# Weight-block sums in a seven-product stage: adding transfers that read DRAM, and another order of the products

## The chip, the core and the metric

The kernel runs on one core of a Trainium2 chip. The core has a matrix engine (TensorE, PE in the profile, with PEld for its weight loads), a vector engine (VectorE, DVE), a scalar engine (ScalarE, ACT), GpSimd (POOL), SyncE (SP), and 16 DMA engines that they all share. Each engine works through its own instructions in order and waits on semaphores for the others. The metric is the device time of one execution in microseconds.

## The reference, cut to what matters

With `DEPTH = 1` the model has one layer: a short gated convolution as token mixer, then a routed mixture of experts. The change lies in the mixer's first product, `h @ w_in`, of 2048 tokens by 1024 channels with a matrix of 1024 by 3072.

```python
def short_conv_mixer(h, w_in, conv_w, w_out):
    gate_b, gate_c, v = jnp.split(h @ w_in, 3, axis=-1)
    return (gate_b * dwconv_centred(gate_c * v, conv_w)) @ w_out

hl = modulate(rms_norm(lat, norm_g[i, 0]), sh1, sc1)
yl = short_conv_mixer(hl, sc_w_in[j], sc_conv[j], sc_w_out[j])
lat = lat + g1 * yl
hl2 = modulate(rms_norm(lat, norm_g[i, 1]), sh2, sc2)
lat = lat + g2 * expert_choice_ffn(hl2, moe_router[i], moe_w_gate[i], moe_w_up[i], moe_w_down[i])
```

## The kernel before

Every float32 factor of a product is split into a high part, rounded to the type `F32R`, and a low part, the rest. A product of two such factors is three matmuls: high by high, low by high, high by low. Tokens go in four quarters of 512 (`QT`).

The first two quarters are multiplied plainly (`in_mm`). The last two are multiplied in a **seven-product stage**, which is the place of the change. It runs over 12 units. A unit takes two column tiles of 128 columns, that is two pieces of `w_in`: piece a and piece b, of 1024 rows by 128 columns each. Their two row halves are (a, 0), (a, 1), (b, 0) and (b, 1), blocks of 512 rows by 128 columns. These four blocks and the four blocks of activations (two quarters by two halves of the channels) form a product of 2 by 2 blocks, which is done with seven block products of sums and differences in place of eight. The seven activation blocks have the names `B11, T1, T2, B21, T3, B22, T4`; they were summed earlier, written to the DRAM scratch `fscr`, and are loaded (tile `fu`) and split (tile `tg`) once for all units, in `refill`, by 14 half groups whose order is `halves`.

One block product is 12 matmuls (`product`): four row tiles, three matmuls each, into one bank of PSUM (`pm`, 128 by 512). In step n of the stage (n = 7 u + i, for product i of unit u) the code writes, in this order: `make_block(n + 4)`, which makes the weight block that is needed four products later (`AHEAD = 4`); whatever `later` holds for step n, mostly parts of the convolution of the unit before (`conv_start`, `conv_rest`, `conv_gate`); in each fourth step an `ada_step`, a slice of another matrix-vector sum (load of `aw` by POOL, addition into `acc` by DVE); and `unit_step`, the product itself and what moves its bank. No scheduler changes this order: each engine takes its instructions as they are written.

`make_block` writes the tile `sb`, whose part 0 is the high part and part 1 the low part. It works on the loaded pieces (`raw`, three buffers, `n_raw`), in place: DVE forms a sum or difference in one half of a piece (L780 to L785), ACT rounds it into part 0 (L786), and the low part is done in one of two ways. For the blocks that need no sum (the unit's products 0, 1 and 4) ACT writes the negated high part into part 1 (L788) and POOL issues a DMA that adds the float32 block from `raw` to it (L789). For the other four DVE subtracts (L791). When the last block of a piece is made, `piece_done` gives its buffer back, and SP issues the load of the piece three further on (L200). The load waits until everything that reads or writes the buffer is through.

The products of a unit share banks: `st[(0, 1, 2, 1, 4, 1, 2)[i]]`. Product 0 keeps a bank for itself until the unit's end, products 1, 3 and 5 add up in a second, 2 and 6 in a third, 4 has a fourth. After products 1, 2, 3 and 5 ACT copies the bank's running sum into one of four quarters of the results x and y (tiles `cx`, `cy`, L847), and a product that goes on in the same bank waits for that copy. DVE adds the rest: one sum after product 4 (L849), three after product 6 (L851 to L853).

Of the kernel before, what the change touches and what calls it, by code (L numbers as in the profile page):

```python
# [13 lines left out]
ALU = mybir.AluOpType  # L14
# [8 lines left out]
KD = D // P  # L23
# [13 lines left out]
N_GROUP = 7  # L37
# [3 lines left out]
def dram(src, offset, ap):  # L41
    return bass.AP(tensor=src.tensor, offset=src.offset + offset, ap=ap)
# [3 lines left out]
def block_kernel(ctx: ExitStack, tc, x, c, ada_w, ada_b, norm_g, w_in, conv, w_out, router, wg, wu, wd, out):  # L46
    nc = tc.nc
# [130 lines left out]
    pieces, n_load, n_high, n_done = [], 6, 6, 6  # L178
# [179 lines left out]
    with tc.tile_pool(name="mix", bufs=1) as mix, ExitStack() as ctx_mixd:  # L358
# [13 lines left out]
        def wide(name, shape=[P, 2 * QT + 4], dt=F32):  # L372
            return cvp.tile(shape, dt, name=name, tag="wide", bufs=6)
# [252 lines left out]
        for g in range(4):  # L626
# [3 lines left out]
            full = scale_x(0, k)  # L630
# [9 lines left out]
            full = scale_x(0, k + 1)  # L640
# [43 lines left out]
            if t + 1 < KD:  # L684
                ada_load(g, t + 1, eng)

        T4, B11, T1, T2, B21, T3, B22 = range(N_GROUP)
        group_of_k = {(2, 0): B11, (2, 1): B21, (3, 1): B22}
        rows_F = {}

# [18 lines left out]
        def save_sums(j):  # L709
# [3 lines left out]
            for h in range(2):  # L713
# [12 lines left out]

        grp, full_of = {}, {}

        halves = [(T4, 0), (T4, 1), (B11, 0), (B11, 1), (T1, 0), (T1, 1), (B21, 0), (B21, 1), (T3, 0), (T3, 1),
                  (T2, 0), (T2, 1), (B22, 0), (B22, 1)]  # L730
        in_big = [(T4, 0), (T4, 1), (B11, 0), (B11, 1), (T1, 0), (T2, 0), (T2, 1), (B22, 0)]

        def load_full(s):
            if s >= len(halves):
# [26 lines left out]
        def raw_half(i, h):  # L761
            return raws[i][:, 4 * h:4 * h + 4]

        def piece_done(i):
            nonlocal n_high, n_done
            raws.pop(i)
            n_high = n_done = i + 1
            load_to(i + depth())
# [3 lines left out]
        def make_block(n):  # L772

            u, i = divmod(n, N_GROUP)
            a, b = first_s + 2 * u, first_s + 2 * u + 1
            t = blk[n] = hl_tile([P, 2, KD // 2, P], name="sb")
            p, h = ((b, 1), (a, 0), (b, 1), (b, 1), (a, 1), (a, 0), (b, 0))[i]
            full = raw_half(p, h)
            if i == 2:
                nc.vector.tensor_add(full, raw_half(b, 0), full)  # L780
            elif i == 3:
                nc.vector.tensor_sub(full, full, raw_half(a, 0))
            elif i == 5:
                nc.vector.tensor_sub(full, full, raw_half(b, 0))
                nc.vector.tensor_sub(raw_half(b, 0), raw_half(a, 1), raw_half(b, 1))  # L785
            nc.scalar.activation(t[:, 0], full, AF.Copy)  # L786
            if i in (0, 1, 4):
                nc.scalar.activation(t[:, 1], t[:, 0].bitcast(F32), AF.Copy, scale=-1.0)  # L788
                nc.gpsimd.dma_start(t[:, 1], full, accum_op=ALU.add)  # L789
            else:  # L790
                nc.vector.tensor_sub(t[:, 1], full, t[:, 0].bitcast(F32))  # L791
            if i > 4:
                piece_done(p)

        def product(o, n, first):
            t, g = blk.pop(n), n % N_GROUP
            for j in range(KD // 2):
                r = grp[g, j]
                last = j == KD // 2 - 1
                nc.tensor.matmul(o, t[:, 0, j], r[:, 0], start=(first and j == 0), stop=False, skip_group_check=True)  # L800
                nc.tensor.matmul(o, t[:, 1, j], r[:, 0], start=False, stop=False, skip_group_check=True)  # L801
                nc.tensor.matmul(o, t[:, 0, j], r[:, 1], start=False, stop=last, skip_group_check=True)  # L802
# [29 lines left out]
        def unit_step(u, i, st):  # L832

            n = N_GROUP * u + i
            if i in (0, 1, 2, 4):
                st[i] = mm.tile([P, QT], F32, name="pm", tag="mm")
            o = st[(0, 1, 2, 1, 4, 1, 2)[i]]
            product(o, n, i in (0, 1, 2, 4))
            if i == 1:
                st["x"] = wide("cx")  # L840
            if i == 2:
                st["y"] = wide("cy")
            x, y = st.get("x"), st.get("y")
            q0, q1 = slice(2, 2 + QT), slice(2 + QT, 2 + 2 * QT)
            if i in (1, 2, 3, 5):
                dst = {1: (x, q0), 2: (y, q1), 3: (x, q1), 5: (y, q0)}[i]
                nc.scalar.activation(dst[0][:, dst[1]], o, AF.Copy)  # L847
            elif i == 4:
                nc.vector.tensor_add(x[:, q0], x[:, q0], o)  # L849
            elif i == 6:  # L850
                nc.vector.tensor_add(y[:, q1], y[:, q1], y[:, q0])  # L851
                nc.vector.tensor_add(y[:, q0], y[:, q0], st[0])
                nc.vector.tensor_add(x[:, q1], x[:, q1], o)  # L853
                (m, ct), (_, ct2) = units[u]
                if m == 0:
                    at(n + 1, lambda: conv_gate(ct, x))
                    at(n + 2, lambda: conv_gate(ct2, y))
                else:
                    convs[ct] = x
                    at(n + 1, lambda: conv_start(ct, x, y))  # L860
                    at(n + 2, lambda: conv_rest(ct, x, y))
# [4 lines left out]
        for i, (ct, q) in enumerate(steps):  # L866
# [10 lines left out]
            for k in range(KD):  # L877
# [14 lines left out]
                if i < 5 and k % 2 == 1:  # L892
                    t = 4 * i + k // 2
# [28 lines left out]
        st = {}  # L922
# [16 lines left out]
        for n in range(n_steps):  # L939
            u, i = divmod(n, N_GROUP)  # L940
# [709 lines left out]
```

## Time and profile before

| | |
|---|---|
| median of 3 runs | 1893.7 us (1890.02 to 1894.17) |
| profiled execution | 1893.85 us, span of its instructions 1892.1 us |
| seven-product stage in it | first matmul at 313.85 us, last at 570.06 us |
| busy over the span | PE 1819.7 us, DVE 1198.5, ACT 893.0, POOL 338.5 |
| mean granted TensorE clock | 0.986 of full |

The profile is of one execution. Times of engines overlap, so busy times don't add up to the span. A matmul's recorded length is longer than its share of the engine, since matmuls are pipelined: what counts is the distance from one start to the next. An idle time in brackets is followed by the instruction that ended it. The stretch of 313.6 to 570.3 us is one seventh of the execution. Of the page's 40 slices TensorE is below 80% busy in the first, the last and the seventeenth (757 to 804 us, where tokens are given to experts); the stage lies in none of them.

### The profile page before, as it was taken

The numbers are of one execution on the slowest core, as the hardware profiler recorded it, in microseconds if no ns is written. First come the engines' busy times: TensorE is split into PE (matmuls) and PEld (weight loads), VectorE is DVE, ScalarE is ACT, GpSimd is POOL, SyncE is SP. The second block draws the span as 40 slices with busy tenths as digits, with TensorE's granted clock in tenths as the row PEclk, the third lists the DMA queues.
The fourth block names the chain that finished last, engine by engine and source line by source line (L and its number), as shares of the span: only waits on it lengthen the run. The fifth ranks groups of instructions, "written<-read, shape, count | busy, mean of one in ns | idle before, by whom it ended". The sixth has DMA issues, their size and how long they took to land.

```text
span 1892.1 us, 29374 instructions
## 1 busy us (share of the span) xinstructions
PE 1819.7 (96%) x11511; PEld 1612.5 (85%) x11511; DVE 1198.5 (63%) x1686; ACT 893.0 (47%) x1190; POOL 338.5 (18%) x514
## 2 busy tenths in 40 slices
PE   7999999998999999499999999999999999999997
PEld 6778887876777888398899999999999999999996
DVE  6554347666667777778656666765666676566653
ACT  4512335433344555566444553544455355445541
POOL 1112232122212222210102102110210221021002
PEclk9999999999999999799999999999999999999999
DMA  9354367656568888386787878788787978877774
GB/s 334 111 190 129 110 226 243 156 139 156 138 170 265 246 261 244 134 258 192 202 251 246 233 223 267 215 244 245 252 228 224 264 221 245 244 250 230 224 229 83
DMA packets 309818, 403.11 MB, mean 213 GB/s; under 512 B 103300, under 2 KB 174256, under 8 KB 309680
## 3 DMA queue, kind: packets, MB, share of 16 engines
q1 hardware_dynamic: 282336, 314.16, 54.4%
q0 software_dynamic: 27344, 87.08, 17.0%
q8 instruction: 90, 1.47, 0.3%
q14 instruction: 48, 0.39, 0.1%
HBM read 311.52 MB, written 57.68 MB: 195 GB/s over the span
## 4 chain that ended last, share of the span: by engine, by line
PE 75%; DMA 7%; DVE 7%; issue 5%; ACT 3%; POOL 1%; SPq 0%; POOLq 0%; DVEq 0%; ACTq 0%
PE pm L1473 11%; PE pm L1475 11%; PE pm L1477 11%; PE pm L1542 6%; PE pm L1540 6%; PE pm L1541 6%; PE pm L488 3%; PE pm L489 3%; PE pm L491 3%; PE pm L1002 3%; PE pm L1003 3%; PE pm L1005 3%; DMA sb<-raw 2%; DMA raw<-in_sc_w_in_dram 1%; DMA tr<-xs 1%
## 5 line engine op out<-in xcount | busy, mean ns | idle before, releaser
L235 DVE TENSOR_TENSOR ws<-raw,ws 128x1024 fp32r<-128x1024 f32 x408 | 485.0, 1221 | 281.5 <-ACT ws L225 281.4
L225 ACT ACTIVATE ws<-raw 128x1024 fp32r<-128x1024 f32 x408 | 412.6, 1051 | 413.4 <-PE pm L1477 323.4
L1473 PE MATMUL pm<-xT,ws 128*128 128x256 f32 x2048 | 568.4, 278 | 0.4 <-ACT xT L1452 0.4
L1475 PE MATMUL pm<-xT,ws 128*128 128x256 f32 x2048 | 567.0, 277 | 1.9 <-DVE xT L1453 1.7
L1477 PE MATMUL pm<-xT,ws 128*128 128x256 f32 x2048 | 566.6, 277 | 0.0
L1475 PEld LDWEIGHTS pm<-xT,ws 128*128 128x128 f32 x2048 | 385.6, 188 | 3.9 <-DVE xT L1453 2.1
L1473 PEld LDWEIGHTS pm<-xT,ws 128*128 128x128 f32 x2048 | 385.2, 188 | 2.0 <-ACT xT L1452 0.8
L1477 PEld LDWEIGHTS pm<-xT,ws 128*128 128x128 f32 x2048 | 385.1, 188 | 0.0
L1570 POOL DMA_INDIRECT out_dram<-ot,idx x30 | 104.7, 3491 | 588.0 <-DVE ot L1559 583.9
L1542 PE MATMUL pm<-ws,hT 128*128 128x512 f32 x504 | 198.4, 394 | 0.0
L1540 PE MATMUL pm<-ws,hT 128*128 128x512 f32 x504 | 198.1, 393 | 0.0
L1541 PE MATMUL pm<-ws,hT 128*128 128x512 f32 x504 | 197.0, 391 | 0.0
L488 PE MATMUL pm<-hl,ws 128*128 128x512 f32 x384 | 154.0, 401 | 0.0
L489 PE MATMUL pm<-hl,ws 128*128 128x512 f32 x384 | 150.7, 392 | 0.0
L800 PE MATMUL pm<-tg,sb 128*128 128x512 f32 x336 | 135.2, 402 | 15.3 <-ACT cx L847 15.2
L801 PE MATMUL pm<-tg,sb 128*128 128x512 f32 x336 | 132.6, 395 | 0.7 <-DMA sb<-raw 0.7
L802 PE MATMUL pm<-tg,sb 128*128 128x512 f32 x336 | 132.3, 394 | 0.0
L1542 PEld LDWEIGHTS pm<-ws,hT 128*128 128x128 f32 x504 | 94.7, 188 | 20.0
L1541 PEld LDWEIGHTS pm<-ws,hT 128*128 128x128 f32 x504 | 94.7, 188 | 19.8
L1540 PEld LDWEIGHTS pm<-ws,hT 128*128 128x128 f32 x504 | 94.7, 188 | 18.7
L491 PE MATMUL pm<-hl,ws 128*128 128x512 f32 x384 | 108.1, 390 | 0.0
L1002 PE MATMUL pm<-ws,hl 128*128 128x512 f32 x256 | 101.8, 398 | 0.8 <-ACT hl L933 0.8
(362 smaller groups left out, 2507.4 us busy)
## 6 DMA issues: line engine op xcount, KB each, us to landing
raw<-in_moe_w_down_dram SPq DMA_DIRECT2D x128, 512.0 KB, 4.6
raw<-in_moe_w_gate_dram SPq DMA_DIRECT2D x126, 512.0 KB, 4.9
raw<-in_moe_w_up_dram SPq DMA_DIRECT2D x126, 512.0 KB, 3.9
raw<-in_sc_w_in_dram SPq DMA_DIRECT2D x42, 512.0 KB, 4.6
xt<-in_x_dram SPq DMA_DIRECT2D x32, 512.0 KB, 6.5
sb<-raw POOLq DMA_DIRECT2D x36, 256.0 KB, 3.9
hl<-in_ada_w_dram SPq DMA_DIRECT2D x32, 256.0 KB, 6.3
aw<-in_ada_w_dram SPq DMA_DIRECT2D x16, 512.0 KB, 5.4
```

Of the source, the lines that this page charges most:

```text
L225: nc.scalar.activation(t[:, 0], raws[n_high], AF.Copy)
L235: (eng or nc.vector).tensor_sub(t[:, 1, ..., s], raw[..., s], t[:, 0, ..., s].bitcast(F32))
L488: nc.tensor.matmul(ps[m], wh, t[:, 0], start=(k == 0), stop=False)
L489: nc.tensor.matmul(ps[m], wl, t[:, 0], start=False, stop=False)
L491: nc.tensor.matmul(ps[m], W(k, m)[0], t[:, 1], start=False, stop=(k == KD - 1))
L1002: nc.tensor.matmul(ps[h], vh[:, k], w[:, 0, half(h)], start=(k == 0), stop=False)
L1473: nc.tensor.matmul(o, w[:, 0, j, c0], xT[:, 0, k], start=(k == 0 and f % 2 == 0), stop=False, skip_group_check=True)
L1475: nc.tensor.matmul(o, w[:, 0, j, c0], xT[:, 1, k], start=False, stop=False, skip_group_check=True)
L1477: nc.tensor.matmul(o, w[:, 1, j, c0], xT[:, 0, k], start=False, stop=(k == KD - 1), skip_group_check=True)
L1540: nc.tensor.matmul(ps[s], h, w[:, 0, j], start=(k == 0), stop=False)
L1541: nc.tensor.matmul(ps[s], h, w[:, 1, j], start=False, stop=False)
L1542: nc.tensor.matmul(ps[s], l, w[:, 0, j], start=False, stop=(k == KD - 1))
```

## The change

`make_block`, `unit_step` and two lists are rewritten; the arithmetic of the stage is the same, in another order.

- The adding DMA of a block without a sum reads the block from `w_in` in DRAM, no longer from the loaded piece. Its source is then four runs of 128 floats for each partition in place of one run of 512 floats.
- The order of the seven products is B11, T1, T2, B21, T3, B22, T4 (it was T4, B11, T1, T2, B21, T3, B22). Their weight blocks are (a, 0); the sum (b, 0) + (b, 1), formed in (b, 0); that minus (a, 0); (a, 1); (b, 1) minus the sum, formed in (a, 0); (a, 1) minus the sum, formed in (b, 0); and (b, 1). Blocks 0, 3 and 6 are those without a sum.
- Three banks in place of four: products 0, 2, 4 and 6 add up in one, 1 and 5 in a second, 3 has a third. ACT copies after products 0, 1, 2, 4 and 6 (five copies, were four), DVE adds after 3, 4 and 5 (three, were four).
- `halves` and `in_big` follow the new order. Loads of pieces are asked for at the same steps as before: after block 5 (piece a) and block 6 (piece b).

```diff
-        T4, B11, T1, T2, B21, T3, B22 = range(N_GROUP)
+        B11, T1, T2, B21, T3, B22, T4 = range(N_GROUP)
...
-        halves = [(T4, 0), (T4, 1), (B11, 0), (B11, 1), (T1, 0), (T1, 1), (B21, 0), (B21, 1), (T3, 0), (T3, 1),
-                  (T2, 0), (T2, 1), (B22, 0), (B22, 1)]
-        in_big = [(T4, 0), (T4, 1), (B11, 0), (B11, 1), (T1, 0), (T2, 0), (T2, 1), (B22, 0)]
+        halves = [(B11, 0), (B11, 1), (T1, 0), (T1, 1), (T2, 0), (T2, 1), (B21, 0), (B21, 1), (T3, 0), (T3, 1),
+                  (B22, 0), (B22, 1), (T4, 0), (T4, 1)]
+        in_big = [(B11, 0), (B11, 1), (T1, 0), (T1, 1), (T2, 0), (B22, 0), (B22, 1), (T4, 0)]
...
-            p, h = ((b, 1), (a, 0), (b, 1), (b, 1), (a, 1), (a, 0), (b, 0))[i]
+            p, h = ((a, 0), (b, 0), (b, 0), (a, 1), (a, 0), (b, 0), (b, 1))[i]
             full = raw_half(p, h)
-            if i == 2:
-                nc.vector.tensor_add(full, raw_half(b, 0), full)
-            elif i == 3:
+            if i == 1:
+                nc.vector.tensor_add(full, full, raw_half(b, 1))
+            elif i == 2:
                 nc.vector.tensor_sub(full, full, raw_half(a, 0))
+            elif i == 4:
+                nc.vector.tensor_sub(full, raw_half(b, 1), raw_half(b, 0))
             elif i == 5:
-                nc.vector.tensor_sub(full, full, raw_half(b, 0))
-                nc.vector.tensor_sub(raw_half(b, 0), raw_half(a, 1), raw_half(b, 1))
+                nc.vector.tensor_sub(full, raw_half(a, 1), full)
+                piece_done(a)
             nc.scalar.activation(t[:, 0], full, AF.Copy)
-            if i in (0, 1, 4):
+            if i in (0, 3, 6):
+                src, offset, ap, _ = pieces[p]
                 nc.scalar.activation(t[:, 1], t[:, 0].bitcast(F32), AF.Copy, scale=-1.0)
-                nc.gpsimd.dma_start(t[:, 1], full, accum_op=ALU.add)
+                nc.gpsimd.dma_start(t[:, 1], dram(src, offset + h * (KD // 2) * ap[1][0], [ap[0], [ap[1][0], KD // 2], ap[2]]),
+                                    accum_op=ALU.add)
             else:
                 nc.vector.tensor_sub(t[:, 1], full, t[:, 0].bitcast(F32))
-            if i > 4:
-                piece_done(p)
+            if i == 6:
+                piece_done(b)
...
-            if i in (0, 1, 2, 4):
+            if i in (0, 1, 3):
                 st[i] = mm.tile([P, QT], F32, name="pm", tag="mm")
-            o = st[(0, 1, 2, 1, 4, 1, 2)[i]]
-            product(o, n, i in (0, 1, 2, 4))
-            if i == 1:
-                st["x"] = wide("cx")
-            if i == 2:
-                st["y"] = wide("cy")
+            o = st[(0, 1, 0, 3, 0, 1, 0)[i]]
+            product(o, n, i in (0, 1, 3))
+            if i < 2:
+                st["xy"[i]] = wide("c" + "xy"[i])
...
-            if i in (1, 2, 3, 5):
-                dst = {1: (x, q0), 2: (y, q1), 3: (x, q1), 5: (y, q0)}[i]
+            if i in (0, 1, 2, 4, 6):
+                dst = {0: (x, q0), 1: (y, q1), 2: (x, q1), 4: (y, q0), 6: (y, q0)}[i]
                 nc.scalar.activation(dst[0][:, dst[1]], o, AF.Copy)
+            if i == 3:
+                nc.vector.tensor_add(x[:, q0], x[:, q0], o)
             elif i == 4:
-                nc.vector.tensor_add(x[:, q0], x[:, q0], o)
+                nc.vector.tensor_add(y[:, q1], y[:, q1], y[:, q0])
+            elif i == 5:
+                nc.vector.tensor_add(x[:, q1], x[:, q1], o)
             elif i == 6:
-                nc.vector.tensor_add(y[:, q1], y[:, q1], y[:, q0])
-                nc.vector.tensor_add(y[:, q0], y[:, q0], st[0])
-                nc.vector.tensor_add(x[:, q1], x[:, q1], o)
```

How the change stands on the engines, at the places that matter. First SP, the loads of four pieces in the middle of the stage, with the semaphores that each waits for (`DMASW` counts DMAs that POOL issued, `DMAHW` those of SP). Before:

```order
L200 DMA raw_2910<-in_sc_w_in_dram 128x8x128 [waits DMAHW0_49,DMAHW4_49,DMASW3_49,DVE_49]
L200 DMA raw_2932<-in_sc_w_in_dram 128x8x128 [waits DMAHW5_49,DMAHW1_49,DVE_49]
L200 DMA raw_3048<-in_sc_w_in_dram 128x8x128 [waits DMAHW6_49,DMASW0_49,DVE_49]
L200 DMA raw_3074<-in_sc_w_in_dram 128x8x128 [waits DMAHW0_49,DVE_49]
```

and the same four loads with the change:

```order
L200 DMA raw_2907<-in_sc_w_in_dram 128x8x128 [waits DMAHW0_49,DMAHW4_49,DVE_49,Activation_49]
L200 DMA raw_2932<-in_sc_w_in_dram 128x8x128 [waits DMAHW1_49,DMAHW5_49,DVE_49,Activation_49]
L200 DMA raw_3044<-in_sc_w_in_dram 128x8x128 [waits DMAHW6_49,DVE_49,Activation_49]
L200 DMA raw_3073<-in_sc_w_in_dram 128x8x128 [waits DMAHW0_49,DVE_49,Activation_49]
```

Before, every second load waits for a DMA of POOL; with the change none does, and each waits for ACT and DVE.

Then ACT, from step 1 of the third unit on. L786 rounds a block and L788 negates it, L847 copies a bank. Before (the first row is block 5, the fourth and fifth are block 0 of the next unit):

```order
L786 ACTIVATE sb<-raw 128x512 [waits DVE_49,PE_49]
L847 ACTIVATE cx<-pm 128x512 [waits PE_49]
L786 ACTIVATE sb<-raw 128x512 [waits DMASW0_49,DVE_49]
L847 ACTIVATE cy<-pm 128x512 [waits DMASW2_49,PE_49]
L786 ACTIVATE sb<-raw 128x512 [waits DMAHW0_49,DMASW2_49]
L788 ACTIVATE sb<-sb 128x512 [waits Activation_49]
L847 ACTIVATE cx<-pm 128x512 [waits PE_49]
L786 ACTIVATE sb<-raw 128x512 [waits DMAHW6_49]
L788 ACTIVATE sb<-sb 128x512 [waits Activation_49]
L786 ACTIVATE sb<-raw 128x512 [waits DVE_49]
```

With the change the two are L788 and L791, the copy is L849 and L820 is the convolution's multiplication. From step 0 of the same unit on (the first row is block 4, the seventh is the negation of block 6):

```order
L788 ACTIVATE sb<-raw 128x512 [waits DVE_49]
L820 ACTIVATE cx<-cy,v_col 128x1025 [waits DVE_49,Activation_49,Pool_49]
L849 ACTIVATE cx<-pm 128x512 [waits PE_49]
L788 ACTIVATE sb<-raw 128x512 [waits DMASW7_49,DVE_49]
L849 ACTIVATE cy<-pm 128x512 [waits DMASW1_49,PE_49]
L788 ACTIVATE sb<-raw 128x512 [waits DMASW0_49]
L791 ACTIVATE sb<-sb 128x512 [waits Activation_49]
L849 ACTIVATE cx<-pm 128x512 [waits PE_49]
L788 ACTIVATE sb<-raw 128x512 [waits DMAHW6_49]
L791 ACTIVATE sb<-sb 128x512 [waits Activation_49]
L788 ACTIVATE sb<-raw 128x512 [waits DMAHW0_49,DVE_49]
```

The copies stand behind other rows than before: the copy of product 0, which product 2 waits for, stands behind the convolution's multiplication. The first block of the next unit (the two rows behind the third copy here and behind the second before) stood ahead of the copy of product 3, and now no copy stands in its step.

Last DVE, from the sum after product 4 (before) and after product 3 (with the change) on, over one unit. Before (L780 to L785 form blocks in `raw`, L791 is a low part, L849 to L853 add banks, L812 is the convolution, L541 the slice of the matrix-vector sum):

```order
L849 TENSOR_TENSOR cx<-cx,pm 128x512 [waits DMASW0_49,PE_49]
L780 TENSOR_TENSOR raw<-raw 128x512 [waits DMASW7_49,DMAHW5_49,DMASW0_49,Activation_49]
L791 TENSOR_TENSOR sb<-raw,sb 128x512 [waits Activation_49]
L782 TENSOR_TENSOR raw<-raw 128x512 [waits DMAHW4_49,DVE_49]
L791 TENSOR_TENSOR sb<-raw,sb 128x512 [waits Activation_49]
L851 TENSOR_TENSOR cy<-cy 128x512 [waits DMASW2_49]
L852 TENSOR_TENSOR cy<-cy,pm 128x512 [waits DVE_49]
L853 TENSOR_TENSOR cx<-cx,pm 128x512 [waits PE_49]
L812 TENSOR_TENSOR cy<-cx,cy 128x1024 [waits DVE_49]
L541 SCALAR_TENSOR_TENSOR acc<-aw,s_col,acc 128x1024 [waits DMASW6_49]
L784 TENSOR_TENSOR raw<-raw 128x512 [waits DMASW2_49]
L785 TENSOR_TENSOR raw<-raw 128x512 [waits DVE_49]
```

With the change L780 to L786 form blocks, L795 is a low part, L851 to L855 add banks and L816 is the convolution:

```order
L851 TENSOR_TENSOR cx<-cx,pm 128x512 [waits DMASW7_49,PE_49]
L780 TENSOR_TENSOR raw<-raw 128x512 [waits DMAHW5_49]
L795 TENSOR_TENSOR sb<-raw,sb 128x512 [waits Activation_49]
L853 TENSOR_TENSOR cy<-cy 128x512 [waits DMASW1_49,Activation_49]
L782 TENSOR_TENSOR raw<-raw 128x512 [waits DMAHW4_49,DVE_49]
L795 TENSOR_TENSOR sb<-raw,sb 128x512 [waits DMASW4_49,Activation_49]
L855 TENSOR_TENSOR cx<-cx,pm 128x512 [waits PE_49]
L784 TENSOR_TENSOR raw<-raw 128x512
L795 TENSOR_TENSOR sb<-raw,sb 128x512 [waits Activation_49]
L816 TENSOR_TENSOR cy<-cx,cy 128x1024
L541 SCALAR_TENSOR_TENSOR acc<-aw,s_col,acc 128x1024 [waits DMASW6_49]
L786 TENSOR_TENSOR raw<-raw 128x512
```

Before, the first sum in a piece waits for two DMAs of POOL (`DMASW`), and the difference of L784 for one; now no row that forms a block waits for a DMA of POOL, only for the loads of pieces. The two last differences, which stood together, lie in two steps.

## Rows read from the trace of the kernel before

**Rows 1.** TensorE's instructions in order of time: the stage's first matmuls, the first long wait, and the stage's end. Columns: start in us, length in us, engine, line, operation, tiles, shapes; in brackets the idle time before it and what ended it.

```profile
313.85 0.39 PE L800 MATMUL pm<-tg,sb 128*128 128x512 f32 x1
...
321.78 0.39 PE L802 MATMUL pm<-tg,sb 128*128 128x512 f32 x1
325.03 0.80 PE L800 MATMUL pm<-tg,sb 128*128 128x512 f32 x1 [2.86 <-ACT cx L847]
...
439.71 1.88 PE L548 MATMUL pt<-acc,ones_f 128*128 128x512 f32 x4
441.03 0.79 PE L800 MATMUL pm<-tg,sb 128*128 128x512 f32 x1
441.66 0.40 PE L801 MATMUL pm<-tg,sb 128*128 128x512 f32 x1
...
570.06 0.39 PE L802 MATMUL pm<-tg,sb 128*128 128x512 f32 x1
```

**Rows 2.** Who waited for whom between 313 and 570.5 us, TensorE's part: total in us, times, longest.

```profile
PE pm L800 <- ACT cx L847: 15.2, 9, 3.5
PE pm L801 <- DMA sb<-raw: 0.7, 1, 0.7
```

**Rows 3.** Busy time of the engines in three stretches: the whole stage and the two stretches behind its longest waits. Columns: stretch, length, then for PE, PEld, DVE, ACT, POOL the busy time and the count, the granted TensorE clock, the share of the DMA engines that is busy, GB/s.

```profile
313.60:570.30 256.70, 240.73 (x1018) 192.59 (x1016) 161.84 (x205) 111.38 (x185) 51.22 (x89) 0.98 0.60 155
...
325.00:328.20 3.20, 3.17 (x8) 2.50 (x9) 2.58 (x3) 2.10 (x4) 0.00 (x0) 0.50 0.69 197
459.00:464.70 5.70, 5.70 (x13) 4.45 (x14) 1.68 (x3) 1.90 (x4) 2.10 (x3) 0.50 0.75 144
```

**Rows 4.** ACT in order of time in the fourth unit, around a late copy.

```profile
388.12 0.63 ACT L786 ACTIVATE sb<-raw 128x512 fp32r<-128x512 f32 x1 [3.29 <-DMA raw<-in_sc_w_in_dram]
388.79 0.63 ACT L788 ACTIVATE sb<-sb 128x512 fp32r<-128x512 f32 x1
389.32 0.58 ACT L847 ACTIVATE cx<-pm 128x512 f32<-128x512 f32 x1
```

**Rows 5.** Who waited for whom between 313 and 571 us, all engines, and SP's own waits in the stage.

```profile
POOL aw L528 <- DVE acc L541: 42.9, 7, 10.2
ACT sb L786 <- DVE raw L780: 42.4, 11, 6.4
DVE raw L780 <- DMA sb<-raw: 37.3, 10, 6.0
ACT sb L786 <- DMA raw<-in_sc_w_in_dram: 30.7, 10, 6.4
...
SPq L200 <- DMA sb<-raw: 169.3, 11, 20.0
```

**Rows 6.** The chain of waits through the stage in order of time, one turn of it. Columns: start, length, what ("issue" is time in which the engine waited for nothing that the profile shows).

```profile
343.03 3.74 DMA raw<-in_sc_w_in_dram
...
348.45 4.15 DMA sb<-raw
...
360.06 1.20 DVE acc L541
...
363.33 4.99 DMA raw<-in_sc_w_in_dram
```

**Rows 7.** Groups of instructions by line in the stage: busy time and mean ns of one, then the idle time before them.

```profile
L791 DVE TENSOR_TENSOR sb<-raw,sb 128x512 fp32r<-128x512 f32 x47 | 32.5, 691 | 19.1 <-ACT sb L786 18.9
L541 DVE SCALAR_TENSOR_TENSOR acc<-aw,s_col,acc 128x1024 f32<-128x1024 f32 x14 | 17.9, 1279 | 0.0
L812 DVE TENSOR_TENSOR cy<-cx,cy 128x1024 f32<-128x1024 f32 x8 | 9.8, 1226 | 0.3
...
L786 ACT ACTIVATE sb<-raw 128x512 fp32r<-128x512 f32 x80 | 49.0, 625 | 102.2 <-DVE raw L780 42.4 <-DMA raw<-in_sc_w_in_dram 30.7 <-DVE raw L784 17.8
L847 ACT ACTIVATE cy<-pm 128x512 f32<-128x512 f32 x24 | 14.2, 591 | 11.4 <-PE pm L802 11.4
L816 ACT ACTIVATE cx<-cy,v_col 128x1025 f32<-128x1025 f32 x8 | 9.2, 1155 | 23.7 <-DVE cy L812 20.9 <-POOL cy L814 2.8
```

**Rows 8.** POOL's issue of the adding DMA (count, ns min/median/max) and the time from its issue to its landing; the longest DMA issue on POOL; then the DMA queues in two short stretches: 297 to 303 us, in which POOL's queue holds adding DMAs only, and 428 to 433.5 us, in which SP's queue loads pieces. Columns of the queues: packets, MB, busy share of the 16 engines.

```profile
L789 POOL DMA_DIRECT2D sb<-raw x36: 857/879/1226, 297.4 to 553.0; - x36
...
DMA to landing us min/median/max: 3.3/3.9/8.5
...
L1570 POOL DMA_INDIRECT out_dram<-ot,idx x30 | 104.7, 3491 | 588.0 <-DVE ot L1559 583.9 <-issue 3.8 <-DVE ws L235 0.3
...
q1 hardware_dynamic: 782, 1.51, 73.3%
q0 software_dynamic: 144, 0.26, 28.2%
...
q1 hardware_dynamic: 1427, 0.72, 45.4%
```

**Rows 9.** POOL's last stores of T1 and T4 to DRAM (L719 and L725) and ACT's splitting of the first activation groups, in order of time ahead of the stage.

```profile
285.04 0.54 POOL L719 DMA_DIRECT2D fscr<-tsum  x1 [0.67 <-DVE tsum L718]
...
287.04 0.54 POOL L725 DMA_DIRECT2D fscr<-fy  x1
...
294.84 1.06 ACT L745 ACTIVATE tg<-fu 128x1024 fp32r<-128x1024 f32 x1 [5.36 <-DMA fu<-fscr]
...
301.23 0.58 ACT L498 ACTIVATE cs<-pm 128x512 f32<-128x512 f32 x1
```

## The prediction

> **What bounds the kernel now.** I read the page's busy shares first: TensorE is at work for 96% of the span, so only places where it waits can give time. Then its own instructions in order of time in the stretch that the change touches [rows 1]. Without waits a matmul starts (321.78 − 313.85) / 35 = 0.2266 us after the one before, so the stage's 1008 matmuls (12 units of 84) need 228.4 us. From its first start to the last one plus one distance it takes 570.06 + 0.23 − 313.85 = 256.4 us. So 28.0 us are lost here, and nothing that the change does to the stage can bring more.
>
> What are the 28.0 us? Twice four matmuls of the matrix-vector sum stand in between; the first time they take 441.03 − 439.71 = 1.3 us and the restart behind them 0.4 us more than a normal distance [rows 1], so about 3.5 us for both, and they stay. TensorE's waits are 15.2 us for a bank's copy by ACT, nine times, and 0.7 us for an adding DMA [rows 2]. The remaining 8.6 us come behind those waits: twice the granted clock is 0.50, the 1.2 GHz level, after TensorE had waited 2.86 us and, the other time, up to 3.5 us (8 starts in 3.2 us and 13 in 5.7 us, where 14 and 25 fit, so 6 and 12 starts or 4.1 us) [rows 1 to 3], and the pipeline starts up again after each wait.
>
> Why is a copy late? A copy takes 0.6 us, and it stands in ACT's queue behind a block's rounding and negation, and the rounding waits itself, here 3.29 us for a piece's load: the copy starts at 389.32 [rows 4]. In the stage that rounding waits 42.4 us for DVE's first sum and 30.7 us for loads; the sum waits 37.3 us for the adding DMA, since it overwrites what the DMA reads; and SP's loads wait 169.3 us for the same DMA, since they overwrite the buffer [rows 5]. So the stage has a loop, and the chain of waits shows a turn of it: load, rounding and negation, adding DMA, sums, next load, 363.33 − 343.03 = 20.3 us [rows 6]. TensorE's own work for a unit is 84 × 0.2266 = 19.0 us. The loop is the longer of the two: **ACT, DVE and the loads set the stage's pace, TensorE waits for them.**
>
> **The change, part by part.** *The adding DMA no longer reads the piece.* With it go DVE's wait, and SP's wait for POOL's DMA (the order rows of SP and DVE show none). The loop that is left, for piece b: load 5.0 us [rows 6]; three sums, each with a rounding and a low part ahead of the next, 3 × (0.70 + 0.64 + 0.70) = 6.1 us; the fourth difference 0.7 us; two additions of banks between them 1.4 us; at worst the convolution's 1.2 us and a slice of the matrix-vector sum of 1.3 us [rows 6 and 7]. Together 15.7 us, against 19.0 us on TensorE. So TensorE becomes the bound, with some 3 us a unit to spare. The first block of a unit now comes from piece a, whose load is asked for a whole unit earlier; piece b is first needed at the unit's second block, three steps (8.2 us) after its load can start. That hides the load; without the cover it would cost what it costs now.
>
> *Three banks.* Products 2, 4 and 6 each wait for the copy of the product two before, so a copy has one product's time, 12 × 0.2266 = 2.72 us, in which to start and end. The narrow place is product 2. Counting from the start of product 0, B: the last copy of the unit before starts at B + 0.2 (its bank must be complete), block 4's rounding at B + 0.7, its low part on DVE at B + 1.4, the convolution's product at B + 2.0 for 1.23 us [rows 7], ACT's convolution row at B + 3.3 for 1.16 us [rows 7], the copy of product 0 at B + 4.5, done at B + 5.1. Product 2 is due at 2 × 2.72 = B + 5.4. **0.3 us are to spare**, in the 8 units of 12 that start a convolution; in the other 4, and for products 4, 5 and 6, 1 us or more. The extra copy per unit (0.6 us of ACT) and the addition less (0.7 us of DVE) lie beside TensorE: ACT is busy for 111 and DVE for 162 of the 257 us [rows 3].
>
> *The DMA's new form.* It has four runs of 512 bytes for each partition, 512 in all, in place of 128 of 2 KB. No row shows an adding DMA of this form, so it is bounded. Busy time of the DMA engines per packet (share × 16 × window / packets): adding 2 KB takes 0.282 × 96 / 144 = 188 ns, plain 2 KB 0.733 × 96 / 782 = 90 ns, plain 512 bytes 0.454 × 88 / 1427 = 28 ns [rows 8]. If adding doubles a small packet as it does a large one, 512 of them need 512 × 58 / 16 = 1.9 us of all engines against 1.5 us now. If a packet keeps 188 ns, they need 6.0 us. I take the first, since plain packets shrink with their bytes. POOL's issue may stay at 0.88 us or grow, up to the 3.49 us of its longest DMA issue [rows 8]; I take the first. What lands when: block 6, the tightest, is negated 2.0 us after its step starts and is needed four products, 10.9 us, after that start. So 8.9 us are there for issue and landing, which take 3.9 us at the median and 8.5 at most now [rows 8], 4.3 at the median by my first value, and 11.0 by the upper ends (3.9 + 4.5 + 2.6).
>
> The Trainium skill speaks against this part (DMA: Bandwidth & Descriptors, section Why small descriptors are slow (HBM only)): transfers within SBUF don't suffer from small descriptors, those with HBM pay some three cycles for each packet, beside a cycle for every 32 bytes. As an estimate from that page, 4 × 19 cycles stand against 67, or 13% more, 1.7 us for 1.5. The plain packets of this trace have 4 × 28 against 90 ns, 24% more; so the row is a bit harsher than the page, and by either this DMA would land in time.
>
> *The start.* Four DVE instructions of the first blocks move, none is added. Ahead of the stage ACT waits 5.36 us for a load of the group T4, which is written to DRAM last and was split first; the splitting that follows pushes the row at 301.23 [rows 9]. With T4 last that wait shrinks, by 3 to 4 us as an estimate (the last of T1, now the fourth half loaded, is written 2.0 us before the last of T4, the second half before) [rows 9]. The first long wait in the stage, 2.86 us, is the end of this backlog, with the clock 4.7 us in all (325.03 − 321.78 − 0.23 = 3.0, and 1.4 + 0.3 behind it). Product 2 now has to wait for a copy a step earlier than product 3 had: without the earlier start I count 3.5 us of waits in the first unit, with it 0.5. I take 1.5.
>
> *The sum.* 228.4 (matmuls) + 3.5 (the other matmuls) + 1.5 (start) + 3 (now and then a copy or an adding DMA that comes late: nine waits of the present kind at a third of their price, bounded by 0 and 8) = 236.4 us, against 256.4 now. That is 20 us less. The profiled execution took 1893.85 us, 0.15 from the median; behind the stage nothing else changes and all moves up. Forecast: **1874 us**. The earliest end, with no wait left but those of the two sets of other matmuls, is 256.4 − 231.9 = 24.5 us less: 1869.
>
> **The rivals.** *Copies stay late.* If ACT's or DVE's queue slips by one more instruction of 1.3 us in product 2's chain, 0.3 us of slack become 1.0 us of wait in 8 units, and half as much again behind the waits (8.6 us now stand beside 15.9): 8 × 1.0 × 1.5 = 12 us of the 20 are lost, 1886. For it: 42.9 us in which POOL's queue stands for DVE's additions [rows 5], with more DMAs behind them. Against it: the two things that now stop ACT, 73 us, are gone.
>
> *The adding DMA is slow; slower than before.* The DMA engines are busy for 0.60 of the stage [rows 3], 154 us, of which 36 adding DMAs make 36 × 1.5 = 54. The other 100 us stay. From 136 ns a packet on (36 × 4.35 + 100 = 256.4) the DMA engines alone fill today's stage, and landing is past its 8.9 us. At 160 ns the stage takes 100 + 36 × 5.1 = 284 us, so 28 us more: 1922. For it: an adding packet reads two places and writes one, and its time may not shrink with its size. Against it: the plain packets do.
>
> *The change doesn't take the wait away.* If a load still waited for something as late as the DMA (ACT's rounding of block 6 is named in its waits now), the loop would stay at 20.3 us or so, and the time at 1894. The order rows speak against it: ACT's row stands well ahead of the DMA's landing.
>
> **How the numbers follow.** Forecast, 1869 to 1880: 0.60. Copies late, 1880 to 1889: 0.16. Better than 1869, by a start that gives more: 0.03. No change, 1890 to 1897: 0.07. Slow DMA, 1898 to 1950: 0.14. About 0.2%, 3.8 us, is what a measurement of this kernel can tell from no change. So faster 0.79, the same 0.07, slower 0.14. The range goes from 1868 to 1892: it holds the forecast, the late copies and the better part of what lies just under no change, 0.8 in all.
>
> **What would show it.** Right: TensorE's waits for copies in the stage fall from 15.2 to under 4 us; the stage takes 232 to 242 us; SP's loads wait for ACT and DVE and not for POOL's DMAs; ACT's rounding waits hardly for loads; no stretch of the stage past its first unit has a clock of 0.50. Wrong: waits of TensorE for the adding DMA, a landing above 8 us at the median, or a busy share of the DMA engines above 0.9 would mean that the new form is dear; waits of product 2 alone, in units that start a convolution, would mean that the narrow place closed.

## The result, and the profile after

| | before | with the change |
|---|---|---|
| median, device us | 1893.5 (1890.02 to 1894.17, 4 runs) | 1871.9 (1869.64 to 1873.80, 4 runs) |
| ratio | 1 | 0.9889, 95% interval 0.9872 to 0.9906 |
| profiled execution, span | 1893.85, 1892.1 | 1871.1, 1869.3 |
| seven-product stage in it | 256.4 | 236.2 |

The profiled executions differ by 22.75 us. The stage is 20.2 us shorter and starts 0.8 us earlier; the other 1.7 us lie behind it, in code that the change doesn't touch.

In the changed kernel L804 to L806 are the stage's matmuls, L788 rounds, L791 negates, L792 is the adding DMA, L795 the low part on DVE, L780 to L786 form blocks, L849 copies a bank, and L816 and L820 are the convolution's rows on DVE and ACT. First TensorE in order of time, as in [rows 1]:

```profile
313.05 0.39 PE L804 MATMUL pm<-tg,sb 128*128 128x512 f32 x1
...
318.26 0.39 PE L806 MATMUL pm<-tg,sb 128*128 128x512 f32 x1
320.49 0.51 PE L804 MATMUL pm<-tg,sb 128*128 128x512 f32 x1 [1.84 <-ACT cx L849]
...
324.71 0.40 PE L806 MATMUL pm<-tg,sb 128*128 128x512 f32 x1
...
431.22 0.39 PE L806 MATMUL pm<-tg,sb 128*128 128x512 f32 x1
431.45 1.88 PE L548 MATMUL pt<-acc,ones_f 128*128 128x512 f32 x4
...
433.39 0.40 PE L805 MATMUL pm<-tg,sb 128*128 128x512 f32 x1
...
549.03 0.39 PE L806 MATMUL pm<-tg,sb 128*128 128x512 f32 x1
549.26 0.39 PE L1005 MATMUL pm<-ws,hl 128*128 128x512 f32 x1
```

The stage lasts 549.26 − 313.05 = 236.2 us, 7.8 more than its matmuls need. One wait is left, for product 2 of the first unit: 324.71 is the twelfth start after 318.26, which takes 12 × 0.2266 = 2.7 us without a wait and took 6.45, so 3.7 us are lost: 1.84 of wait, and the rest at the restart and at a granted clock of 0.50, the 1.2 GHz level, from 321.07 to 324.47. The two sets of L548 cost 1.72 us each (433.39 − 431.22 − 2 × 0.2266 for the first). That leaves 0.7 us (7.8 − 3.7 − 3.4), as the stretches show: the whole stage, in which TensorE is idle for 1.84 us (236.21 − 234.37), the stretch at the lower clock, and three stretches without any idle time (columns as in [rows 3]).

```profile
313.05:549.26 236.21, 234.37 (x1018) 191.65 (x1016) 153.78 (x196) 119.93 (x195) 67.06 (x90) 0.99 0.74 170
...
321.07:324.47 3.40, 3.40 (x10) 2.63 (x9) 2.71 (x5) 1.34 (x2) 1.30 (x2) 0.50 0.22 79
...
336.17:432.00 95.83, 95.83 (x423) 79.11 (x422) 62.64 (x79) 48.70 (x81) 29.79 (x39) 1.00 0.75 168
432.00:452.00 20.00, 20.00 (x87) 16.03 (x86) 12.39 (x17) 8.51 (x15) 6.21 (x10) 1.00 0.85 223
452.00:549.26 97.26, 97.26 (x427) 79.75 (x425) 62.00 (x76) 48.48 (x77) 25.67 (x36) 1.00 0.72 167
```

Who waits for whom in the stage, the lines that answer to [rows 2, 5]:

```profile
ACT sb L788 <- DVE raw L780: 25.4, 11, 3.0
...
PE pm L804 <- ACT cx L849: 1.8, 1, 1.8
...
SPq L200 <- DVE raw L786: 163.4, 12, 17.5
SPq L200 <- DVE sb L795: 17.1, 12, 2.0
...
SPq L200 <- ACT sb L788: 10.4, 13, 1.6
```

TensorE's nine waits of 15.2 us have become one of 1.8, ACT's 30.7 us for loads and DVE's 37.3 us for the adding DMA are gone, and SP's loads of pieces (L200) wait for no DMA of POOL. But these loads still wait for 191 us in all, now for DVE and ACT: keep this for the second experiment.

ACT in order of time at the narrow place, in the unit whose product 0 starts at B = 355.29:

```profile
355.49 0.60 ACT L849 ACTIVATE cy<-pm 128x512 f32<-128x512 f32 x1 [1.66 <-PE pm L806]
355.98 0.62 ACT L788 ACTIVATE sb<-raw 128x512 fp32r<-128x512 f32 x1
358.58 1.16 ACT L820 ACTIVATE cx<-cy,v_col 128x1025 f32<-128x1025 f32 x1 [1.98 <-DVE cy L816]
359.64 0.58 ACT L849 ACTIVATE cx<-pm 128x512 f32<-128x512 f32 x1
```

The copy of product 0 is done at 360.22, B + 4.93, and product 2 starts at B + 5.44 without a wait: 0.5 us to spare. The adding DMA: POOL's issue and the time to landing, then POOL's queue from 312 to 319 us, in which it holds one adding DMA and little else (columns as in [rows 8]).

```profile
L792 POOL DMA_DIRECT2D sb<-in_sc_w_in_dram x36: 1269/1297/1859, 295.4 to 537.9; - x36
...
DMA to landing us min/median/max: 4.3/5.2/8.6
...
q0 software_dynamic: 528, 0.26, 30.4%
```

A packet takes 0.304 × 16 × 7 / 528 = 64.5 ns, so one such DMA 512 × 64.5 / 16 = 2.1 us of all engines (1.5 before), and POOL's issue 1.30 us at the median (0.88 before). Last the start, ACT in order of time as in [rows 9]:

```profile
293.79 0.63 ACT L788 ACTIVATE sb<-raw 128x512 fp32r<-128x512 f32 x1 [2.87 <-DMA fscr<-fx]
...
296.81 1.06 ACT L745 ACTIVATE tg<-fu 128x1024 fp32r<-128x1024 f32 x1 [0.78 <-DMA fu<-fscr]
299.82 0.63 ACT L788 ACTIVATE sb<-raw 128x512 fp32r<-128x512 f32 x1 [1.94 <-DVE raw L780]
...
301.30 0.58 ACT L498 ACTIVATE cs<-pm 128x512 f32<-128x512 f32 x1
```

The one wait of 5.36 us has become three of 2.87, 0.78 and 1.94, and the row behind them stands at 301.30, where it stood at 301.23. The first of the three is a block's rounding, and the profile puts its wait down to POOL's store of an activation sum (`fscr<-fx`): the tiles `fx` and `sb` take turns in the same buffers (`hl_tile`). The second is for a load, the third for DVE's first sum.

### The profile page after: what moved, and what is told of

It reads as the page before. It is cut to its first block, busy times and chain, and to the rows that moved or that the text cites. A ratio compares the mean times of both kernels' runs of the same rounds, so it can differ in the third digit from the quotient of the medians.

```text
span 1869.3 us, 29368 instructions
## 1 busy us (share of the span) xinstructions
PE 1812.7 (97%) x11511; PEld 1611.4 (86%) x11511; DVE 1187.7 (64%) x1674; ACT 901.4 (48%) x1202; POOL 355.7 (19%) x514
## 4 chain that ended last, share of the span: by engine, by line
PE 87%; DVE 4%; DMA 3%; issue 3%; ACT 2%; POOL 1%; POOLq 0%; SPq 0%; DVEq 0%; ACTq 0%
PE pm L1476 12%; PE pm L1478 12%; PE pm L1480 12%; PE pm L1545 6%; PE pm L1543 6%; PE pm L1544 6%; PE pm L804 4%; PE pm L806 4%; PE pm L805 4%; PE pm L488 3%; PE pm L489 3%; PE pm L491 3%; PE pm L1005 3%; PE pm L1008 3%; PE pm L1006 3%
## 5 line engine op out<-in xcount | busy, mean ns | idle before, releaser
L804 PE MATMUL pm<-tg,sb 128*128 128x512 f32 x336 | 132.6, 395 | 1.8 <-ACT cx L849 1.8
L806 PE MATMUL pm<-tg,sb 128*128 128x512 f32 x336 | 131.5, 391 | 0.0
L805 PE MATMUL pm<-tg,sb 128*128 128x512 f32 x336 | 131.3, 391 | 0.0
L1417 POOL DMA_INDIRECT xs<-hhalf,idx x30 | 43.0, 1432 | 317.2 <-issue 228.3
```

## The experiments

The theory: a loop that takes longer than TensorE's unit (20.3 us in the turn of [rows 6]), closed by the sum that overwrites a block which an adding DMA still reads, set the pace; the change opens it, and TensorE then runs at its own 19.0 us. Its rivals: the gain is of the banks and copies, or of SP's loads coming earlier, or of the start. Each run shared its runs of the kernel before with the others of its group (medians 1892.93 us for the first four, 1891.41 for the last four).

**The source alone.** The kernel before, with only the adding DMA's source in DRAM.

```diff
-                nc.gpsimd.dma_start(t[:, 1], full, accum_op=ALU.add)
+                src, offset, ap, _ = pieces[p]
+                nc.gpsimd.dma_start(t[:, 1], dram(src, offset + h * (KD // 2) * ap[1][0], [ap[0], [ap[1][0], KD // 2], ap[2]]),
+                                    accum_op=ALU.add)
```

> The kernel before with the adding DMA reading w_in in DRAM, and nothing else changed: old order of products, four banks. Theory (the loop through the adding DMA set the pace): without the DMA the turn is load 3.7, a rounding 0.6 and the 10.7 us of sums that were counted from 352.68 to 363.33, about 15 us, under TensorE's 19.0, so this part alone ends the loop. Stage 234 to 242 us, time 1872 to 1880, most of the change's 22 us. Rival (the new order does it, since piece b is wanted a step later): the first block of a unit still waits for its load, stage 246 to 256 us, time 1884 to 1894.

Measured: 1874.45 us (1872.62 to 1875.62), ratio 0.9897 (0.9881 to 0.9914). The stage takes 238.6 us. TensorE has one wait, in the first unit, here at product 3; all later units run at 19.04 us but for L548.

```profile
325.47 0.80 PE L802 MATMUL pm<-tg,sb 128*128 128x512 f32 x1 [3.56 <-ACT cx L849]
```

So the order and the three banks are not needed for the gain in the later units; the 2.4 us by which this stage is longer than the changed kernel's lie in the first.

**The order alone.** The changed kernel, with the DMA's source in the loaded piece as before.

```diff
-                nc.gpsimd.dma_start(t[:, 1], dram(src, offset + h * (KD // 2) * ap[1][0], [ap[0], [ap[1][0], KD // 2], ap[2]]),
-                                    accum_op=ALU.add)
+                nc.gpsimd.dma_start(t[:, 1], full, accum_op=ALU.add)
```

> The changed kernel with the adding DMA reading the loaded piece again: new order and three banks alone. Theory: with the lower right block last, no sum overwrites what a DMA has just begun to read, and piece a's load follows block 6's DMA by a whole unit of slack, so the order alone ends the loop as well. Stage 234 to 239 us, time 1870 to 1876. Rival (the source in DRAM is needed): SP's loads wait for the DMA as before and the stage stays at 246 to 256 us, time 1884 to 1894.

Measured: 1871.54 us (1870.90 to 1877.21), ratio 0.9894 (0.9873 to 0.9915); the stage takes 236.8 us. SP's waits in it, then the stage as a stretch, then POOL's issue and landing:

```profile
SPq L200 <- DMA sb<-raw: 170.8, 21, 11.7
```

```profile
313.30:550.10 236.80, 232.75 (x1018) 190.49 (x1017) 153.62 (x196) 120.56 (x197) 52.61 (x90) 1.00 0.65 169
```

```profile
L791 POOL DMA_DIRECT2D sb<-raw x36: 858/880/1213, 295.2 to 538.8; - x36
...
DMA to landing us min/median/max: 3.2/3.8/7.2
```

SP's loads wait for the adding DMAs as long in all as before the change (169.3 us then), and the gain is there in full: TensorE has two waits left, of 2.41 and 1.64 us, both in the first unit. In the new order the unit's first block comes from piece a, and no sum overwrites it until block 4 is formed, four products later. Each part of the change opens the loop by itself, and the second one adds nothing that can be measured. The stage's DMA share is 0.65 here and 0.74 with the DRAM source: 0.09 × 236.5 / 36 = 0.6 us of all engines for each adding DMA, as 2.1 against 1.5 from the packets.

**One DMA less.** The kernel before, its order and source kept; only the low part of each unit's first block is formed by DVE in place of the negation and the DMA.

```diff
-            if i in (0, 1, 4):
+            if i in (1, 4):
```

> The kernel before, but the low part of each unit's first block (the lower right block, whose buffer the next sum overwrites) is a subtraction on DVE in place of ACT's negation and the adding DMA; the other two adding DMAs of a unit stay, reading the piece. Theory: this one DMA closes the loop; without it the turn is about 16 us, so stage 236 to 246 us, time 1873 to 1884, although neither the source nor the order changed. Rival (all reads of the pieces by DMAs hold the loads up alike, or the late loads themselves do): a third of the gain at most, stage 249 to 256, time 1887 to 1894.

Measured: 1875.17 us (1872.61 to 1878.60), ratio 0.9904 (0.9885 to 0.9924); the stage takes 238.4 us, with a wait at product 3 of the first unit and no other. SP's wait for DMAs that read pieces is still there.

```profile
327.89 0.79 PE L800 MATMUL pm<-tg,sb 128*128 128x512 f32 x1 [4.65 <-ACT cx L847]
```

```profile
SPq L200 <- DMA sb<-raw: 150.0, 11, 16.0
```

Of 36 adding DMAs the 12 of the units' first blocks closed the loop. Taking those away gives what either part gives. The edit also takes 12 negations from ACT; the source alone keeps them and has the same gain.

**The narrow place, closed on purpose.** The changed kernel, with two multiplications by 1.0 behind the convolution's product on DVE.

```diff
             nc.vector.tensor_mul(o, c[:, 2:2 + 2 * QT], o)
+            nc.vector.tensor_scalar(o, o, 1.0, None, op0=ALU.mult)
+            nc.vector.tensor_scalar(o, o, 1.0, None, op0=ALU.mult)
```

> The changed kernel with two more DVE instructions (times 1.0, over 1024 elements in place) right behind the convolution's product in the 8 units that start one; results don't change. They lengthen the chain to the copy of product 0 by 1.3 us. Theory (that chain is the narrow place, with 0.3 us to spare by the prediction and 0.5 us by the trace of the changed kernel): TensorE waits 0.8 to 1.2 us at product 2 in each of the 8 units, stage 6 to 12 us longer than the changed kernel's, time 1878 to 1884. Rival (the chain is not tight): under 2 us longer, 1870 to 1874.

Measured: 1881.3 us (1879.91 to 1881.76), ratio 0.9943 (0.9928 to 0.9958), and its interval lies above that of the changed kernel. The stage takes 244.7 us, 8.5 more. DVE's two added rows, ACT's row of the convolution and the copy behind it, then TensorE, in the same unit as above, whose product 0 starts at B = 356.40 here:

```profile
359.61 0.69 DVE L817 TENSOR_SCALAR cy<-cy 128x1024 f32<-128x1024 f32 x1
360.34 0.70 DVE L818 TENSOR_SCALAR cy<-cy 128x1024 f32<-128x1024 f32 x1
...
361.15 1.16 ACT L822 ACTIVATE cx<-cy,v_col 128x1025 f32<-128x1025 f32 x1 [3.44 <-DVE cy L818]
362.21 0.58 ACT L851 ACTIVATE cx<-pm 128x512 f32<-128x512 f32 x1
```

```profile
361.62 0.39 PE L806 MATMUL pm<-tg,sb 128*128 128x512 f32 x1
362.84 0.50 PE L804 MATMUL pm<-tg,sb 128*128 128x512 f32 x1 [0.84 <-ACT cx L851]
```

ACT's row of the convolution starts at B + 4.75 in place of B + 3.29, 1.46 us later. Of that 0.5 is the slack, and product 2 starts 1.0 us late (362.84 − 361.62 − 0.23), of which the profile shows 0.84 as idle time. In the eight units that start a convolution TensorE loses 1.1 to 1.5 us at product 2, 9.2 in all. In three of the other four it loses nothing there, and in the first unit, which waits in the changed kernel too, 0.7. The place, its slack and about its price are as the prediction put them.

**The first unit's wait.** What of it is due to `in_out`, which ends the plain product of the last columns and is called in step 0? The changed kernel, with that call in step 3, and, in a second kernel, in step 5.

```diff
-        at(0, lambda: in_out(*pend))
+        at(3, lambda: in_out(*pend))
```

> The changed kernel with the rest of the plain half's last tile (the call of in_out for the pending banks) written at step 3 of the stage in place of step 0. Theory: the 3.7 us lost at the first unit's product 2 come from ACT's and DVE's rows of that call and the splitting, ahead of the copy of product 0; without the call there the copy is in time, and the time is 3 to 4 us under the changed kernel's, 1867 to 1869. Rival (the backlog is of the splitting of activation groups, which stays): under 1 us of difference, 1871 to 1873.

> The changed kernel with the call of in_out for the plain half's last tile at step 5 in place of step 0 (step 3 only moved the first unit's wait on to product 6, since the call's five rows on DVE then stood ahead of the sum that block 1 of the next unit needs). Theory: at step 5 its DVE rows stand where DVE has some 2.5 us to spare a unit and no copy with a product behind it follows on ACT, so the first unit's 3.7 to 6 us go for the most part. Stage 232 to 234 us, time 1867 to 1870. Rival (the backlog of the splitting itself is the bound, wherever the call stands): the wait shows up at another product and the time stays at 1871 to 1874.

Measured: step 3 takes 1873.5 us (1872.81 to 1874.14), ratio 0.9896 (0.9879 to 0.9912); step 5 takes 1873.1 us (1871.82 to 1877.63), ratio 0.9902 (0.9887 to 0.9917). The stage takes 238.3 us in both. TensorE with step 3, and with step 5:

```profile
335.00 0.64 PE L804 MATMUL pm<-tg,sb 128*128 128x512 f32 x1 [3.87 <-ACT cy L849]
```

```profile
342.85 0.80 PE L804 MATMUL pm<-tg,sb 128*128 128x512 f32 x1 [4.09 <-ACT cx L849]
```

With step 3 product 2 is in time and product 6 of the same unit waits; with step 5 the first unit is clean and product 2 of the second unit waits. Each time the copy stands in ACT's queue behind a row that waits for DVE or POOL, and the call's rows stand ahead of those. With step 3, on DVE:

```profile
331.25 0.15 DVE L519 COPY carry<-pm 128x1 f32<-128x1 f32 x1
331.32 1.28 DVE L753 TENSOR_TENSOR tg<-fu,tg 128x512 fp32r<-128x512 f32 x2
332.52 0.68 DVE L851 TENSOR_TENSOR cx<-cx,pm 128x512 f32<-128x512 f32 x1
333.12 0.68 DVE L780 TENSOR_TENSOR raw<-raw 128x512 f32<-128x512 f32 x1
```

So my theory, that the wait goes when the call comes later, fell. In these two kernels the wait follows the call. Whether the call or the splitting beside it (L753) is what has to give way isn't settled.

**The new form, with less cover.** Blocks are made two products ahead in place of four, once with the DRAM source and once with the source in the piece (the second of these is the order alone with the same edit). Fewer blocks are then made ahead of the stage as well.

```diff
-AHEAD = 4
+AHEAD = 2
...
-                    if k in (4, 5):
-                        make_block(k - 2)
...
-        W_LOADS, W_SPLITS = (3, 2), {3: 0, 1: 2, 0: 3}
+        W_LOADS, W_SPLITS = (3, 2), {2: 0, 1: 2, 0: 3}
```

> The changed kernel with blocks made two products ahead in place of four (and the first split of an output weight one step later, which this needs). Takes away the cover of the adding DMA: block 6 is negated 2.0 us after its step starts and needed 5.6 us after it, so 3.6 us are left for issue and landing, which take 5.2 us at the median. Theory: TensorE waits for the adding DMA at products 0, 3 and 6 of each unit, about 1.5 to 3 us each, stage 50 to 100 us longer, 1920 to 1970. Rival (the new form is cheap enough at any distance): under 20 us longer.

> The same with the adding DMA reading the loaded piece, so new order, blocks two products ahead, the form of before (landing 3.8 us at the median). Theory: the price of the new form shows once its cover is gone. Its landing is 1.4 us longer, and each of 36 blocks waits that much less here: 30 to 55 us under the kernel that reads DRAM two products ahead. Rival: no difference beyond 10 us, the form costs nothing even uncovered.

Measured: with the DRAM source 1926.64 us (1924.63 to 1929.35), ratio 1.0186 (1.0171 to 1.0202), stage 288.5 us; with the source in the piece 1910.12 us (1904.78 to 1914.80), ratio 1.0089 (1.0066 to 1.0112), stage 274.3 us. TensorE's waits for the adding DMA, in the first and in the second:

```profile
PE pm L805 <- DMA sb<-in_sc_w_in_dram: 40.7, 25, 6.6
```

```profile
PE pm L803 <- DMA sb<-raw: 28.0, 16, 4.5
```

Two products ahead, the DRAM source costs 16.5 us (14.2 of them in the stage), less than the theory's 30 to 55 and more than the rival's 10; the runs of the second kernel spread over 10 us, so the size is rough. Four products ahead, no wait of TensorE for it is left in the stage.

No kernel tried was faster than the changed one by more than the intervals; the order alone stands level with it.

## Why the prediction was right, point by point

*What bounds the kernel.* Right, and shown: three different edits that open the loop at its first block each shorten the stage by 18 to 20 us. One step of the argument proved nothing, though. I put SP's 169.3 us for the DMA among the loop's waits [rows 5]. The order alone keeps 170.8 us of them and has the gain. What counted was DVE's sum that waited for the same DMA (37.3 us before, and in none of the three kernels), with ACT's rounding and then the copies behind it. The length of the loop was read from one turn, and a short one. In the rows below DVE forms the first sum of a piece (L780): before the change, nine turns apart, and with it, one turn apart:

```profile
352.68 0.69 DVE L780 TENSOR_TENSOR raw<-raw 128x512 f32<-128x512 f32 x1 [0.62 <-DMA sb<-raw]
...
548.01 0.69 DVE L780 TENSOR_TENSOR raw<-raw 128x512 f32<-128x512 f32 x1 [1.31 <-DMA sb<-raw]
```

```profile
405.05 0.69 DVE L780 TENSOR_TENSOR raw<-raw 128x512 f32<-128x512 f32 x1
424.09 0.69 DVE L780 TENSOR_TENSOR raw<-raw 128x512 f32<-128x512 f32 x1
```

Before, a turn took 21.7 us on average ((548.01 − 352.68) / 9), where the prediction has 20.3; with the change it takes 19.04. TensorE's own time, with the two sets of L548 that fall into the nine turns, is 19.4 us a turn, and nine times the difference of 2.3 us are 20.6, about the whole gain.

*The matmuls and L548.* 228.4 and 3.4 us, where 228.4 and 3.5 were predicted.

*The start.* This term was mis-sized: 1.5 us taken (0.5 to 3.5), 3.7 measured. The step that failed is that ACT's wait for T4 shrinks by 3 to 4 us and the rest moves forward. The wait for the groups' loads did shrink, but two others (2.87 us, by the profile for the store of an activation sum, and 1.94 us for DVE's first sum) filled the place, and the row behind stayed at 301.3. Without an earlier start the prediction counted 3.5 us of waits in the first unit; 3.7 were lost, of them 1.84 of wait and the rest at the restart and the lower clock.

*Late copies and DMAs later in the stage.* 3 us taken (0 to 8), about 0.7 measured (7.8 − 3.4 − 3.7). The 3 us don't follow from their own words either: a third of nine waits of 15.2 us is 5.1. This term and the start have errors of opposite sign, so the stage's 236.2 us against the 236.4 forecast is closer than the working deserved: that is luck.

*Three banks.* 0.3 us to spare predicted, 0.5 found. The rival "copies stay late" had the right place: 1.39 us of added DVE work made it come true, with 9.2 us lost at the eight places and a stage 8.5 us longer, where its formula gives 8 × 0.84 × 1.5 = 10.1.

*The DMA's new form.* Dearer than I took it, within the bounds, and hidden: 64.5 ns a packet for 58, landing 5.2 us for 4.3, POOL's issue 1.30 us for 0.88. The prediction's point at which the rival "slow DMA" decides, 136 ns, is twice what was measured. For the same bytes, 4 × 64.5 against 188 ns is 37% more, from one stretch of each kernel; the source changed with the packets, from the loaded piece to DRAM. The plain packets of the prediction gave 24%. The Trainium skill (DMA: Bandwidth & Descriptors, section Why small descriptors are slow (HBM only)) puts a fixed cost of some three cycles on each packet, which as the prediction's estimate made 13%. That has the right sign and is too low; the measurement decides. The dearer form doesn't show in the time here, since the blocks are made four products ahead.

*The rest.* "Behind the stage nothing else changes" is off by 1.7 us, of the size by which executions of one kernel differ. The forecast of 1874 was 2 us too high.

## What to carry to other kernels

When an engine waits for copies or buffers, add up a turn of the loop behind the wait, over several turns, and set it against the bound engine's own time for the same unit of work; here the loop was 2.3 us longer on average, which over nine turns is about the gain, and opening it in one place was enough. A queue that waits long is no evidence by itself: SP waited some 170 us in the order alone, as it did before the change. And after such a repair, look for the place that is narrow now and measure its slack by adding a known amount of work: 0.5 us here, where a row that came 1.5 us later made TensorE 1.0 us late.

## What the runs showed of the hardware that was not expected

- An adding DMA in 512-byte packets from DRAM costs POOL 1.30 us to issue and one in 2 KB packets from a loaded piece 0.88 us, for the same 256 KB: the issue grows by 0.42 us with 384 packets more.
- In the changed kernel TensorE waited 1.84 us in the first unit, took up its matmuls again, and from 321.07 to 324.47 the granted clock was 0.50, the 1.2 GHz level. In the order alone a wait of 2.41 us at the same product was followed by a granted clock of 1.00, the 2.4 GHz level, over 3.7 us, and in the kernel before one of 2.70 us by 1.00 over 3.9 us. So these longer waits kept the clock, and the shorter one lost it, as one of 2.86 us in the kernel before did [rows 1, 3]; why is open. TensorE's restart and the stretch behind it, in the order alone and in the kernel before:

```profile
321.32 0.50 PE L802 MATMUL pm<-tg,sb 128*128 128x512 f32 x1 [2.41 <-ACT cx L847]
```

```profile
321.32:325.00 3.68, 3.68 (x16) 3.07 (x17) 2.95 (x6) 1.04 (x2) 1.50 (x3) 1.00 0.19 71
```

```profile
428.14 0.50 PE L800 MATMUL pm<-tg,sb 128*128 128x512 f32 x1 [2.70 <-ACT cx L847]
```

```profile
428.14:432.00 3.86, 3.86 (x17) 3.21 (x18) 3.75 (x5) 0.95 (x2) 0.00 (x0) 1.00 0.47 136
```
